# A hybrid Fourier/SSD transformer layer on Trainium2: PSUM tiles of the channel products, the DFT table's memory, and the opening of the last feed-forward block

## The chip, the cores and the metric

The kernel runs on one core of a Trainium2 chip (trn2). A core has five engines that work side by side, each through its own queue of instructions: TensorE (PE, matmuls, with its weight loads shown as PEld), VectorE (DVE), ScalarE (ACT), GpSimd (POOL) and SyncE (SP), which here issues the DMA transfers. The metric is the device time of one execution in microseconds (us); lower is better. The kernel before takes 2312.03 us, the median of three runs (2309.56, 2312.03 and 2312.89).

## The reference, cut to what matters

One layer works on 1024 latent tokens and 256 context tokens of width 1024, with the same weights for both, in float32:

```
def macaron_ffn(x, mod3, norm_pre, norm_post, w_gate, w_up, w_down):
    h = modulate(rms_norm(x, norm_pre), mod3[:, 0], mod3[:, 1])
    y = (jax.nn.silu(h @ w_gate) * (h @ w_up)) @ w_down
    return x + MACARON_WEIGHT * mod3[:, 2][:, None, :] * rms_norm(y, norm_post)

def mix_sublayer(...):
    h = modulate(rms_norm(x, norm_pre), mod3[:, 0], mod3[:, 1])
    u_f, z, xbc, dt_raw = jnp.split(h @ w_in, [...], axis=-1)
    xbc = centred_dwconv_silu(xbc, conv_w, conv_b)
    ...                                  # two directions of an SSD scan, y = y_f + flip(y_b) + ...
    out = jnp.concatenate([fourier_mix(u_f, fourier_w), y], axis=-1) @ w_out
    return x + mod3[:, 2][:, None, :] * rms_norm(out, norm_post), h_f, h_b

def fourier_mix(u, fourier_w):
    uh = u.reshape(b, L, FOURIER_HEADS, FOURIER_HEAD_DIM).astype(jnp.float32)
    f = jnp.fft.fft2(uh, axes=(1, 3), norm='ortho').real.astype(u.dtype)
    return jnp.einsum('blhd,hde->blhe', f, fourier_w).reshape(b, L, FOURIER_WIDTH)
```

The latent tokens pass a feed-forward block (hidden width 2816), the mixing block and a second feed-forward block. The context tokens pass the first feed-forward block and the mixing block's projection, which give the SSD scan its starting states. The vectors of `modulate` and the gates come from adaLN products of the two conditioning vectors.

## The kernel before, in words

**Precision.** A float32 product is taken as three products of halves in a faster format (fp32r): `split` (L194) casts the high half on ScalarE (L198) and subtracts it on VectorE for the low half (L199); `mm3` (L456) issues high times high, high times low and low times high. Nearly all matmuls of the trace therefore carry L461. The matmuls of the DFT (L1240) stay plain float32, and each of them shows as two in the trace.

**Order.** The code is written for a tile framework whose scheduler plays the program on a model of the engines and deals out each engine's queue from that; the queue that results can differ from the written order. Within an engine the queue is fixed. SBUF is handed out by an allocator of areas (`m.alloc`, `m.free`, `Ring` for areas used in turn) in several regions (F0, Q, X1, X2, R0; the trace shows them as F, Q1a, X3a, X3b, R and so on). A load into an area that had another use before waits for the last reader of that memory, so the place of an area sets how early a load can run. PSUM tiles are named by tags (`self.banks`): a product takes the next tile of its tag and waits until that one has been emptied.

**Stages, in the order of the program.**
- First feed-forward block (`ffn1`). The gate and up products are formed in units by a scheme of seven products per unit (`units`, `uload`, `usums`, `usplit`, `product`, `u_first`, `u_mid`, `u_late`, driven by `ffn_up`, L611). A unit loads raw weights (`uload`, L527), forms sums of them on VectorE (`usums`, L534 to L537) and splits them in three groups A11, S1 and S4 (`usplit`). The token side has such sums too: h^T of the latent tokens is held in blocks and sums of blocks. `ffn_down` (L669) then multiplies with the down weights for token tiles 0 and 1, then 2 to 4, then 5 to 7; `down_prep` (L654) loads and splits one group of down weights and gated activations ahead. After a token tile's last matmul comes its norm (`post`, L904, the last step at L793).
- Projection (`project`, L951). First the channel products: 24 blocks of 24 matmuls into `pch` tiles, emptied by ScalarE or VectorE. The banks are dealt out at L963, two one-bank tiles for tag GU and two for AUX beside two larger ones. Between the blocks the rest of the adaLN runs (`ada`, L699): 48 loads of 256 KB into a ring of three areas, sums over them on VectorE (L771), and for every eight loads a cast on ScalarE (L715) and a pair of `pmod` matmuls (L722, L723). Then come the token products `pz`.
- SSD and context (`ssd_and_ctx`, L1354): the scan over chunks of the latent tokens beside the context's feed-forward block, whose products (`gu`, `y`) fill TensorE between the scan's steps. The Fourier part (`fourier`, L1167) is stepped among them; its table for the last step of the DFT is loaded into one area of 4 x 1024 columns (`tw`) and is used at L1240. Then follow the context's norm and transposes (L806, L816), and its projection (`pdt`, `pch`).
- Mixing output (`mix_out`, L1510), where the blocks of h^T for the second feed-forward block are made and partly stored in DRAM (`h_d`).
- Second feed-forward block (`ffn2`, L1648). One pair of hidden blocks is done by plain gate and up products (`gu`), while the stored blocks of h^T are loaded back, summed on VectorE (L396 to L399) and split (L422). Then the units of `ffn_up` follow as in the first block, with products into `pa`, `pb`, `pc` and `pd`, and the last down product (`y`).

Of the kernel before, what the change touches and what calls it, by code (L numbers as in the profile page):

```python
# [7 lines left out]
F32 = mybir.dt.float32  # L8
# [3 lines left out]
ALU = mybir.AluOpType  # L12
AX = mybir.AxisListType

D = 1024
# [112 lines left out]
class Kernel:  # L128
# [423 lines left out]
    def product(self, u, p, steps=range(4)):  # L552
        m = self.m
        tag = {1: "A", 2: "A", 6: "B", 5: "C", 3: "C", 7: "D", 4: "D"}[p]
# [4 lines left out]
        for i in steps:  # L559
            lh, ll = self.wop(wop, i)  # L560
            rh, rl = (m.r(q) for q in self.hop[hop][i])
            self.mm3([P], lh, ll, [rh], [rl], p in (1, 6, 5, 7) and i == 0, i == 3, p != 6)
# [47 lines left out]
    def ffn_up(self, begun, tail, step=lambda: None):  # L610

        n = len(self.ulist)
        for u in range(n):
            if u or not begun:
# [19 lines left out]
            if u > (1 if begun else 0):  # L634
# [34 lines left out]
    def ffn_down(self, post, step=lambda p, f: None, before=lambda p: None):  # L669
# [12 lines left out]
        for p, ts in enumerate(self.passes):  # L682
            for fs in [(0, 1)] + [(f,) for f in range(2, NF - 2)] + [(NF - 2, NF - 1)]:
# [6 lines left out]
                for i, t in enumerate(ts):  # L690
# [141 lines left out]
    def ffn1(self):  # L832
# [71 lines left out]
        def post(t, P):  # L904
            self.rs = V if t > 5 else nc.gpsimd
# [8 lines left out]
        self.ffn_down(post, step, before)  # L914
# [36 lines left out]
    def project(self):  # L951
# [11 lines left out]
        self.banks(main=2, GU=2, AUX=2)  # L963
# [203 lines left out]
    def fourier(self):  # L1167
# [32 lines left out]
        m.free(bd, fw, cs, *u)  # L1200
        s = [m.alloc(256) for _ in range(4)]
        zr = []
        for c in range(2):
            zr.append(m.alloc(2048))
            pq3 = m.f(pq[c]).rearrange("p (t x) -> p t x", x=256)
            z4 = m.f(zr[c]).rearrange("p (r i q x) -> p r i q x", r=4, i=2, q=2)
            for i in range(2):
# [6 lines left out]
                flat = m.f(zr[c]).rearrange("p (r i x) -> p r i x", r=4, i=2)  # L1214
                G.tensor_tensor(out=flat[:, 0, i], in0=s02, in1=s13, op=ALU.add)
                G.tensor_tensor(out=flat[:, 2, i], in0=s02, in1=s13, op=ALU.subtract)
                dd, d1 = (q.rearrange("p (q x) -> p q x", q=2) for q in (d02, d13))
                V.tensor_tensor(out=z4[:, 1, i, 0], in0=dd[:, 0], in1=d1[:, 1], op=ALU.subtract)
                V.tensor_tensor(out=z4[:, 1, i, 1], in0=dd[:, 1], in1=d1[:, 0], op=ALU.add)
                V.tensor_tensor(out=z4[:, 3, i, 0], in0=dd[:, 0], in1=d1[:, 1], op=ALU.add)  # L1220
                V.tensor_tensor(out=z4[:, 3, i, 1], in0=dd[:, 1], in1=d1[:, 0], op=ALU.subtract)
# [3 lines left out]
        tw = m.alloc(4096)  # L1225
        for r in range(4):
            self.load(tw, a["dft"][r], 1024 * r, 1024 * r + 1024)
        fo = [m.alloc(1024, F32, self.F0) for _ in range(2)]
        yield
        for c in range(2):  # L1230
            z4 = m.f(zr[c]).rearrange("p (r i q x) -> p r i q x", r=4, i=2, q=2)
# [619 lines left out]
```

## Time and profile before

| what | value |
|---|---|
| median of three runs | 2312.03 us (2309.56 to 2312.89) |
| the profiled execution | 2308.27 us, its span 2306.3 us |
| mean granted TensorE clock | 0.974 of full speed |
| TensorE busy (PE) | 2151.5 us, 93% of the span |
| weight loads (PEld) | 1795.3 us, 78% |
| VectorE (DVE) | 1500.8 us, 65% |
| ScalarE (ACT) | 922.3 us, 40% |
| GpSimd (POOL) | 410.9 us, 18% |

Times inside the profile are microseconds from the start of the span. An engine is busy while one of its instructions runs; issuing a DMA is not counted. The granted clock is that of TensorE as the chip's throttle allowed it, 1 being full speed (2.4 GHz), 0.5 the lower level (1.2 GHz), and a value between the two a mean over a stretch. A wait is the idle time of an engine before an instruction, put down to what released that instruction last.

### The profile page before, as it was taken

Reading aid. Unit: us, or ns where it says so; the run is one execution under the profiler, and the core shown is the slowest. Engines: PE = TensorE matmul, PEld = TensorE weight load, DVE = VectorE, ACT = ScalarE, POOL = GpSimd, SP = SyncE. Lnnn points to the kernel's source line nnn. Section 1 sums busy time; section 2 is a strip of 40 time slices with the busy share of each in tenths; the row PEclk is TensorE's granted clock in tenths of the full one; section 3 lists DMA queues with packets and bytes.
Section 4 is the critical chain, followed back from the end, with each engine's and each line's share of the span. In section 5 each row is a group of like instructions: output and inputs, shape, how many; then the busy total and the mean of one; then the engine's idle time right before and its main releaser. Section 6 shows DMA issues by size and latency. Waiting matters only on the chain.

```text
span 2306.3 us, 28361 instructions
## 1 busy us (share of the span) xinstructions
PE 2151.5 (93%) x10532; PEld 1795.3 (78%) x10532; DVE 1500.8 (65%) x2231; ACT 922.3 (40%) x1403; POOL 410.9 (18%) x439
## 2 busy tenths in 40 slices
PE   5899999999999899989989978888799999999998
PEld 3688888888878899878878867676688888878886
DVE  6888887655555743358888857786655565656453
ACT  4332323235454414336555545355222222245341
POOL 0000000002030100026866631773000000001010
PEclk9999999999999999999999989999899999999999
DMA  6244444247665742123445445453422221258572
GB/s 263 89 128 135 137 133 135 78 165 257 201 205 175 218 126 92 60 77 106 137 145 167 127 157 165 152 175 121 137 76 91 74 85 68 88 190 285 173 231 89
DMA packets 124826, 329.38 MB, mean 143 GB/s; under 512 B 12928, under 2 KB 43776, under 8 KB 123664
## 3 DMA queue, kind: packets, MB, share of 16 engines
q1 hardware_dynamic: 124688, 327.57, 43.6%
q8 instruction: 83, 1.36, 0.2%
q14 instruction: 55, 0.45, 0.1%
HBM read 273.77 MB, written 53.76 MB: 142 GB/s over the span
## 4 chain that ended last, share of the span: by engine, by line
PE 72%; DVE 10%; DMA 8%; issue 4%; ACT 3%; POOL 3%; SPq 0%; DVEq 0%; POOLq 0%; ACTq 0%
PE y L461 21%; PE pa L461 10%; PE pc L461 10%; PE pd L461 10%; PE pb L461 5%; PE pch L461 5%; PE pz L461 3%; PE gu L461 3%; DMA X3b<-adaR 1%; DVE R L199 1%; PE pwo L461 1%; DVE F L1311 1%; DMA F<-ffn_w 1%; DMA X2a<-ada 1%; POOL R L1265 1%
## 5 line engine op out<-in xcount | busy, mean ns | idle before, releaser
L198 ACT CAST R<-F 128x1024 fp32r<-128x1024 f32 (+1 forms) x172 | 164.7, 963 | 258.2 <-PE pd L461 75.4
L199 DVE TENSOR_TENSOR R<-F,R 128x1024 fp32r<-128x1024 f32 (+1 forms) x155 | 194.7, 1260 | 92.5 <-ACT R L198 85.4
L207 POOL TENSOR_SCALAR F<-F 128x1 f32<-128x1 f32 x18 | 3.7, 206 | 1307.9 <-ACT F L228 1307.7
L198 ACT CAST Q1a<-F 128x1024 fp32r<-128x1024 f32 (+1 forms) x114 | 128.8, 1132 | 209.7 <-PE pd L461 85.8
L461 PE MATMUL pch<-R 128*128 128x512 f32 (+1 forms) x912 | 171.5, 347 | 11.2 <-DVE F L948 6.4
L461 PE MATMUL gu<-R 128*128 128x256 f32 (+1 forms) x1152 | 164.9, 302 | 8.8 <-DVE X5a L512 6.2
L461 PEld LDWEIGHTS pch<-R 128*128 128x128 f32 x912 | 147.1, 195 | 31.6 <-DVE F L948 5.3
L461 PEld LDWEIGHTS gu<-R 128*128 128x128 f32 x1152 | 153.1, 197 | 17.2 <-DVE X5a L512 7.3
L199 DVE TENSOR_TENSOR Q1a<-F,Q1a 128x1024 fp32r<-128x1024 f32 x92 | 112.3, 1221 | 33.7 <-ACT Q1a L198 33.1
L1265 POOL TENSOR_TENSOR R<-F 128x384 fp32r<-128x384 f32 x128 | 126.3, 1015 | 21.7 <-PE pD L1299 15.1
L461 PE MATMUL y<-Q1a 128*128 128x512 f32 x432 | 105.4, 392 | 0.7 <-DVE Q1a L199 0.3
L461 PE MATMUL pa<-R 128*128 128x512 f32 x306 | 86.6, 399 | 12.6 <-ACT R L198 12.1
L461 PEld LDWEIGHTS y<-Q1a 128*128 128x128 f32 x432 | 80.5, 188 | 18.8 <-DVE Q1a L199 0.8
L198 ACT CAST X7a<-F 128x1024 fp32r<-128x1024 f32 (+1 forms) x48 | 58.9, 1229 | 90.1 <-PE pd L461 78.4
L461 PE MATMUL pa<-R,Q1a 128*128 128x512 f32 x330 | 92.9, 394 | 0.0
L461 PE MATMUL y<-Q1a,X3a 128*128 128x512 f32 x348 | 86.8, 396 | 0.0
L461 PE MATMUL pc<-R,Q1a 128*128 128x512 f32 x286 | 85.3, 391 | 0.0
L461 PE MATMUL pd<-R,Q1a 128*128 128x512 f32 x286 | 84.0, 391 | 0.0
L461 PE MATMUL y<-X7a 128*128 128x512 f32 x330 | 79.4, 396 | 2.9 <-ACT X7a L198 2.9
L199 DVE TENSOR_TENSOR X7a<-F,X7a 128x1024 fp32r<-128x1024 f32 (+1 forms) x48 | 69.4, 1446 | 18.5 <-ACT X7a L198 17.6
L461 PEld LDWEIGHTS pa<-R 128*128 128x128 f32 x306 | 58.5, 192 | 27.0 <-ACT R L198 12.5
L534 DVE TENSOR_TENSOR F<-F 128x1024 f32<-128x1024 f32 x42 | 51.4, 1225 | 41.8 <-DMA F<-ffn_w 41.5
(427 smaller groups left out, 4922.2 us busy)
## 6 DMA issues: line engine op xcount, KB each, us to landing
F<-ffn_wd SPq DMA_DIRECT2D x154, 512.0 KB, 4.8
F<-ffn_w SPq DMA_DIRECT2D x42, 1024.0 KB, 5.4
X3b<-adaR SPq DMA_DIRECT2D x96, 256.0 KB, 2.8
F<-ffn_w SPq DMA_DIRECT2D x44, 512.0 KB, 4.2
F<-w_ch SPq DMA_DIRECT2D x26, 512.0 KB, 4.4
g_d<-X3b SPq DMA_DIRECT2D x22, 512.0 KB, 2.8
g_d<-F SPq DMA_DIRECT2D x20, 512.0 KB, 2.6
X3b<-g_d SPq DMA_DIRECT2D x44, 192.0 KB, 5.0
```

The lines of the kernel that those rows point to most:

```text
L198: nc.scalar.copy(out=m.r(hi, off, off + n), in_=m.f(src, soff, soff + n))
L199: (E or nc.vector).tensor_tensor(out=m.r(lo, off, off + n), in0=m.f(src, soff, soff + n), in1=m.f(hi, off, off + n), op=ALU.subtract)
L207: V.tensor_scalar(out=mv, in0=ss, scalar1=scale * RSQ_M, scalar2=EPS * RSQ_M, op0=ALU.mult, op1=ALU.add)
L461: self.nc.tensor.matmul(out=outs[c], lhsT=l, rhs=r[c], start=first and ps == 0, stop=last and ps == 2, skip_group_check=again)
L534: V.tensor_tensor(out=m.f(e).rearrange("p (s c) -> p s c", s=2), in0=s[1].unsqueeze(1).broadcast_to([128, 2, 512]), in1=m.f(w, 0, 2048).re ...
L1265: G.tensor_tensor(out=m.r(R, 384 * i, 384 * i + 384).rearrange("p (h l) -> p h l", h=3), in0=self.cst(tri).unsqueeze(1).broadcast_to([128, ...
L1311: V.scalar_tensor_tensor(out=w, in0=m.f(cb, 512 + 128 * g, 640 + 128 * g), scalar=self.dtT[:, c, 12 + h : 13 + h], in1=w, op0=ALU.mult, op ...
```

## The change

Four places are rewritten.

1. In the channel products the six banks that the two large tiles and GU held together become six one-bank tiles of tag GU (AUX keeps two). In the last pass of the first down product the token tiles of the first step are taken in the order 7, 5, 6, and the reciprocal root of tile 5's norm is computed on VectorE, where POOL did it before.
2. In the Fourier part the two operands of the DFT and its table are held in four pieces each. Two pieces of the table are loaded as soon as the first operands of the Fourier part are freed, the other two where memory of the SSD scan becomes free; the outputs `fo` move to region Q.
3. In the second feed-forward block the raw area of the first unit is allocated, and its load issued, ahead of the blocks of h^T that are read back. `h_sums` is written out in place, over 2560 columns where it used 3584. The first unit takes its products in the order 1, 2, 3, 6, 5, 7, 4, with product 3 in a tile of its own (tag AUX). Products 1, 2 and 3 are those that read h^T's own blocks and the sums of weights that go with them, and the rest read the sums of blocks.
4. Before the last down product three groups are prepared where two were, and the areas for them come from other places.

```
-        self.banks(main=2, GU=2, AUX=2)
+        self.banks(GU=6, AUX=2)
...
-            self.rs = V if t > 5 else nc.gpsimd
+            self.rs = V if t > 4 else nc.gpsimd
...
-        self.ffn_down(post, step, before)
+        self.ffn_down(post, step, before, 2)
...
         m.free(bd, fw, cs, *u)
+        tw = [m.alloc(1024) for _ in range(2)]
+        for r in range(2):
+            self.load(tw[r], a["dft"][r])
...
-            zr.append(m.alloc(2048))
+            zr.append([m.alloc(512) for _ in range(4)])
...
-        tw = m.alloc(4096)
-        for r in range(4):
-            self.load(tw, a["dft"][r], 1024 * r, 1024 * r + 1024)
-        fo = [m.alloc(1024, F32, self.F0) for _ in range(2)]
+        tw += [m.alloc(1024) for _ in range(2)]
+        for r in range(2, 4):
+            self.load(tw[r], a["dft"][r])
+        fo = [m.alloc(1024, F32, self.Q) for _ in range(2)]
...
-        hb = [m.alloc(3584, F32, F0) for _ in range(2)]
+        self.raw = Ring(m, 2560, 1, F32, F0)
+        self.units("ffn2", 1)
+        self.uload(0)
+        hb = [m.alloc(2560, F32, F0) for _ in range(2)]
...
-        self.raw = Ring(m, 2560, 2, F32, F0)
-        self.we = m.alloc(1024, F32, F0)
+        self.raw.areas.append(m.alloc(2560, F32, F0))
+        self.we = m.alloc(1024, F32, X2)
...
+            if u == 0 and not begun:
+
+                self.product(0, 1)
+                self.U[0] = self.ut.next()
+                U = self.m.f(self.U[0])
+                self.nc.scalar.copy(out=U, in_=self.P[0, "A"])
+                self.product(0, 2)
+                P3 = self.P[0, "X"] = self.psum("px", "AUX")
+                self.product(0, 3, tag="X")
...
-            self.down_prep()
-            self.down_prep()
+            self.graw.areas.append(m.alloc(384, F32, F0))
             self.down_begin("ffn2", ((0, 1), (2, 3, 4), (5, 6, 7)))
+            for _ in range(3):
+                self.down_prep()
```

TensorE's queue at the end of the channel products, from the fifth `pmod` pair on; `pch` is a channel product's tile, `pmod` the adaLN product's, `pz` the first token product's. Before:

```order
L461 MATMUL pch<-R_60 128x256 x7
L722 MATMUL pmod<-Q1a,R_60 128x512
L461 MATMUL pch<-R_60 128x256 x6
L723 MATMUL pmod<-Q1a,R_60 128x512
L461 MATMUL pch<-R_60 128x256 x35
L461 MATMUL pch<-R_60,X3a 128x256 x36
L722 MATMUL pmod<-Q1a,R_60 128x512
L461 MATMUL pch<-R_60,X3a 128x256 x6
L723 MATMUL pmod<-Q1a,R_60 128x512
L461 MATMUL pch<-R_60,X3a 128x256 x54
L461 MATMUL pz<-Q1a,R_60 128x408 x192
```

The same place after:

```order
L461 MATMUL pch<-R_60 128x256 x17
L755 MATMUL pmod<-Q1a,R_60 128x512
L461 MATMUL pch<-R_60 128x256 x6
L756 MATMUL pmod<-Q1a,R_60 128x512
L461 MATMUL pch<-R_60 128x256 x25
L461 MATMUL pch<-R_60,X3a 128x256 x47
L755 MATMUL pmod<-Q1a,R_60 128x512
L461 MATMUL pch<-R_60,X3a 128x256 x6
L756 MATMUL pmod<-Q1a,R_60 128x512
L461 MATMUL pch<-R_60,X3a 128x256 x43
L461 MATMUL pz<-Q1a,R_60 128x408 x192
```

The pairs of `pmod` stand further back among the channel products: 54 matmuls were left behind the last pair and 43 are now. At the first pair it is 110 matmuls ahead of it, where there were 101.

TensorE's queue at the DFT: `y` is the context's down product, `pdft` the DFT's tiles, `ptr` the transposes of the context's two token blocks, `pst` products of the scan's states, `pdt` the first product of the context's projection. Before:

```order
L1336 MATMUL pst<-Q4a 128x192 x4
L1240 MATMUL pdft<-Q4a,X5a 128x256 x15
L816 MATMUL ptr<-F_61 128x128 x8
L1240 MATMUL pdft<-Q4a,X5a 128x256 x15
L816 MATMUL ptr<-F_61 128x128 x8
L1240 MATMUL pdft<-Q4a,X5a 128x256 x2
L461 MATMUL pdt<-R_60 24x256
```

After:

```order
L461 MATMUL y<-R_60 128x512 x8
L1275 MATMUL pdft<-X5a 128x256 x5
L1275 MATMUL pdft<-F_61,X5a 128x256 x2
L1371 MATMUL pst<-Q4a 128x192
L1275 MATMUL pdft<-F_61,X5a 128x256 x2
L1371 MATMUL pst<-Q4a 128x192
L1275 MATMUL pdft<-F_61,X5a 128x256 x4
L1371 MATMUL pst<-Q4a 128x192 x2
L1275 MATMUL pdft<-X5a 128x256 x8
L1275 MATMUL pdft<-F_61,X5a 128x256 x4
L849 MATMUL ptr<-F_61 128x128 x8
L1275 MATMUL pdft<-F_61,X5a 128x256 x4
```

Three `pdft` matmuls (not shown) now stand among the `y` products ahead of these rows, and 28 of the 32 stand before the first row of transposes shown; the first two pieces of the table are in X5a and the others in F.

VectorE's queue at the opening of the last feed-forward block, where `gu` is a tile of the plain gate and up products. L396 to L399 are the sums of h^T before, L1707 to L1710 after, and the splits of them are L422 before and L199 (into X7a) after. Before:

```order
L422 TENSOR_TENSOR X7a<-F_61,X7a 128x2048
L1682 TENSOR_TENSOR F_61<-gu,F_61 128x512
L422 TENSOR_TENSOR X7a<-F_61,X7a 128x2048
L534 TENSOR_TENSOR F_61<-F_61 128x1024
L536 TENSOR_TENSOR F_61<-F_61 128x512
L537 TENSOR_TENSOR F_61<-F_61 128x512
L199 TENSOR_TENSOR R_60<-F_61,R_60 128x1024 x2
L534 TENSOR_TENSOR F_61<-F_61 128x1024
L199 TENSOR_TENSOR X7a<-F_61,X7a 128x1536
```

The same place after:

```order
L1708 TENSOR_TENSOR F_61<-F_61 128x512
L199 TENSOR_TENSOR R_60<-F_61,R_60 128x1024
L1709 SCALAR_TENSOR_TENSOR F_61<-F_61 128x512
L199 TENSOR_TENSOR R_60<-X7b,R_60 128x1024
L1707 TENSOR_TENSOR F_61<-F_61 128x512
L1727 TENSOR_TENSOR F_61<-gu,F_61 128x512
L1710 TENSOR_TENSOR F_61<-F_61 128x512
L1708 TENSOR_TENSOR F_61<-F_61 128x512
L1709 SCALAR_TENSOR_TENSOR F_61<-F_61 128x512
L1710 TENSOR_TENSOR F_61<-F_61 128x512
L199 TENSOR_TENSOR X7a<-F_61,X7a 128x2048 x2
L199 TENSOR_TENSOR X7a<-F_61,X7a 128x1536
```

The first unit's weight sums (L534 to L537) have moved up, before these rows, among the last transposes of the mixing output. Its two splits into R stood behind the last split of h^T and now stand among the last sums of h^T. The split of group S4 (1536 columns) still ends the stretch.

## Rows read from the trace of the kernel before

**Rows 1.** Busy time by stretch: start:end, us, busy us (instructions), PEclk, DMA share, GB/s.

```profile
753.00:844.00 91.00, 80.19 (x614) 77.58 (x615) 62.97 (x114) 29.57 (x60) 5.74 (x6) 0.94 0.64 197
1030.00:1340.00 310.00, 275.82 (x1796) 251.06 (x1796) 259.17 (x380) 173.73 (x308) 210.43 (x189) 0.95 0.42 135
1353.00:1380.00 27.00, 18.90 (x83) 15.81 (x82) 12.10 (x31) 15.94 (x26) 7.84 (x5) 0.81 0.66 207
1641.50:1659.30 17.80, 5.23 (x14) 3.72 (x15) 14.29 (x14) 6.45 (x8) 0.00 (x0) 0.62 0.43 136
2057.70:2289.50 231.80, 231.75 (x998) 188.60 (x999) 113.77 (x131) 91.01 (x129) 16.95 (x35) 0.99 0.63 201
```

**Rows 2.** Waits of PE, 749 to 844: waited for, us in total, times, longest.

```profile
PE pch L461 <- ACT F L992: 5.6, 2, 4.5
PE pch L461 <- DVE X3b L793: 3.9, 1, 3.9
```

**Rows 3.** Timeline of PE, channel products: start, us, instruction, count [idle before, releaser].

```profile
752.90 7.50 PE L461 MATMUL pch<-R 128*128 128x256 f32 x48 [3.87 <-DVE X3b L793]
...
802.92 5.92 PE L461 MATMUL pch<-R 128*128 128x256 f32 x48
...
840.87 3.08 PE L461 MATMUL pch<-R,X3a 128*128 128x256 f32 x24 [0.93 <-ACT X3b L995]
```

**Rows 4.** Timeline of DVE and ACT, 755 to 836.

```profile
757.47 1.28 DVE L793 SCALAR_TENSOR_TENSOR X3b<-y,F,X3b 128x1024 f32<-128x1024 f32 x1 [2.88 <-DMA x_d<-X3b]
...
774.40 0.62 ACT L715 CAST Q1a<-F 128x512 fp32r<-128x512 f32 x1 [1.88 <-DVE F L771]
...
834.32 0.62 ACT L715 CAST Q1a<-F 128x512 fp32r<-128x512 f32 x1 [4.02 <-DVE F L771]
```

**Rows 5.** Timeline of all engines at the DFT, 1348 to 1381.

```profile
1348.94 0.32 SPq L1325 DMA_DIRECT2D y_d<-F  x1
...
1359.04 9.51 PE L1240 MATMUL pdft<-Q4a,X5a 128*128 128x256 f32 x30 [5.84 <-DMA Q4a<-dft]
...
1362.50 1.15 ACT L806 ACTIVATE F<-X5a,F 128x1024 f32<-128x1024 f32 x1 [0.61 <-DVE F L214]
...
1369.26 6.64 PE L1240 MATMUL pdft<-Q4a,X5a 128*128 128x256 f32 x30
...
1375.74 1.04 PE L816 MATMUL ptr<-F 128*128 128x128 f32 x8
...
1379.89 0.30 PE L461 MATMUL pdt<-R 128*24 128x256 f32 x1 [2.25 <-ACT R L828]
```

**Rows 6.** Timeline of PE and DVE at the last block's opening, 1630 to 1662.

```profile
1630.08 11.40 PE L461 MATMUL gu<-R,X7a 128*128 128x512 f32 x48
...
1636.46 0.69 DVE L396 TENSOR_TENSOR F<-F 128x512 f32<-128x512 f32 x1 [6.09 <-DMA F<-h_d]
...
1644.59 2.28 DVE L422 TENSOR_TENSOR X7a<-F,X7a 128x2048 fp32r<-128x2048 f32 x1
...
1652.88 2.35 DVE L199 TENSOR_TENSOR R<-F,R 128x1024 fp32r<-128x1024 f32 x2
...
1653.59 1.22 PE L461 MATMUL pa<-R 128*128 128x512 f32 x2 [12.11 <-ACT R L198]
...
1655.29 3.92 PE L461 MATMUL pa<-R 128*128 128x512 f32 x10 [0.48 <-DVE R L199]
...
1656.29 1.75 DVE L199 TENSOR_TENSOR X7a<-F,X7a 128x1536 fp32r<-128x1536 f32 x1
...
1660.43 1.57 PE L461 MATMUL pb<-X7a,R 128*128 128x512 f32 x6
```

**Rows 7.** A link of the chain that ended last: start, us, what.

```profile
1644.11 6.09 DMA F<-ffn_w
```

**Rows 8.** Timeline of PE at the start of the last down product.

```profile
2057.74 7.27 PE L461 MATMUL y<-X7a 128*128 128x512 f32 x24 [2.87 <-ACT X7a L198]
```

**Rows 9.** Longest wait of PE, 1030 to 1340.

```profile
PE gu L461 <- DVE X5a L512: 6.2, 1, 6.2
```

More of the change, by code (lines that the diff above doesn't have):

```diff
@@ L550, in wop, with product @@
         return [self.m.r(q, o, o + 128) for q in self.wq[g]]
-    def product(self, u, p, steps=range(4)):
+    def product(self, u, p, steps=range(4), tag=None):
         m = self.m
-        tag = {1: "A", 2: "A", 6: "B", 5: "C", 3: "C", 7: "D", 4: "D"}[p]
+        tag = tag or {1: "A", 2: "A", 6: "B", 5: "C", 3: "C", 7: "D", 4: "D"}[p]
         if p in (1, 6, 5, 7) and steps[0] == 0:
@@ L613, in ffn_up @@
         for u in range(n):
-            if u or not begun:
+            if u == 0 and not begun:
[6 more added lines that the diff above has]
+                self.product(0, 3, tag="X")
+                V = self.nc.vector
+                s, d = self.u_dest(0)
+                self.u_end(0, 0, s, d)
+                self.product(0, 6)
+                V.tensor_tensor(out=U, in0=self.P[0, "B"], in1=U, op=ALU.add)
+                self.usums(1)
+                self.usplit(1, "A11")
+                for p in (5, 7):
+                    self.product(0, p)
+                self.u_mid(0)
+                V.tensor_tensor(out=self.m.f(d[1]), in0=self.P[0, "C"], in1=U, op=ALU.add)
+                V.tensor_tensor(out=self.m.f(d[1]), in0=P3, in1=self.m.f(d[1]), op=ALU.add)
+                self.u_end(0, 1, s, d)
+                self.product(0, 4)
+                V.tensor_tensor(out=self.m.f(d[2]), in0=self.P[0, "D"], in1=U, op=ALU.add)
+                self.u_end(0, 2, s, d)
+                self.usplit(1, "S1")
+                self.usplit(1, "S4")
+                self.uload(2)
+                continue
+            if u:
                 for p in (1, 6):
@@ L667, in down_prep, with ffn_down @@
         self.ready[q] = (wh, wl, gh, gl)
-    def ffn_down(self, post, step=lambda p, f: None, before=lambda p: None):
+    def ffn_down(self, post, step=lambda p, f: None, before=lambda p: None, turned=0):
         m = self.m
@@ L689, in ffn_down @@
                     self.down_prep()
-                for i, t in enumerate(ts):
+                order = list(enumerate(ts))
+                if p == 2 and fs[0] == 0:
+                    order = order[turned:] + order[:turned]
+                for i, t in order:
                     for f in fs:
@@ L1714, in ffn2 @@
             r.release()
-        m.free(self.cc, wb, lb, h0, l0, h1, l1, *(x for q in T[1:] for x in q), *(m.sub(x, 768, 1280) for x in T[0]))
-        self.pairs(Q, 2, 0)
-        self.pairs(X1, 3, 4)
-        self.graw.areas += [m.alloc(384, F32, X2) for _ in range(2)]
+        m.free(self.cc, wb, lb, h0, l0, h1, l1, *(x for q in T[2:] for x in q),
+               *(m.sub(x, o, n) for q, o, n in ((0, 0, 512), (0, 1664, 384), (1, 0, 512), (1, 1536, 512)) for x in T[q]))
+        self.pairs(R0, 2, 0)
+        self.pairs(X1, 2, 3)
+        self.graw.areas.append(m.alloc(384, F32, X2))
         x = Ring(m, 1024, 2, F32, F0)
```

42 lines of the change are left out of this document (23 added, 19 removed).

## The prediction, made before the changed kernel ran

> **What bounds the kernel now.** I read the page's list by engine first (TensorE is busy 93% of the span), then busy time by stretch, then the waits of TensorE in the stretches where it is not full, and last the timeline there. The reader is to see in the stretches that TensorE is full where the two feed-forward blocks run in steady state (231.75 of 231.8 us in the last one) and is not full in four places: the channel products of the projection, the state-space part, the DFT with the context's last norm, and the opening of the last feed-forward block [rows 1]. Only there can the edits give anything; no matmul is taken away, so the whole effect is idle TensorE time, and the slow clock behind it.
>
> **The change part by part.**
>
> *First channel products (L963 before).* Six one-bank tiles in place of two. TensorE waits here 5.6 us for ACT and 3.9 for DVE to empty tiles [rows 2]. With six tiles these waits can go; that the tiles now taken first are token tile 5's, and that its reciprocal root is computed on VectorE, lets the first product start near 749.0, where TensorE now falls idle (752.90 less 3.87 [rows 3]). But what ends last is another chain: the adaLN vectors, 48 loads through a ring of three buffers into VectorE sums. Its casts for the modulation products come at 774.40 for the first and 834.32 for the sixth [rows 4], so one every (834.32 - 774.40)/5 = 12.0 us. A channel product's matmul takes 5.92/48 = 0.123 us [rows 3], and 71 to 87 of them stand between two modulation pairs in either order, 10.7 us at most. TensorE is therefore ahead of that chain already, and will be further ahead: 110 matmuls (13.5 us) now stand before the first pair, so it gets there about 11 us early and waits. The stretch ends with the last pair plus what stands behind it: 54 matmuls before, 43 now, 11 x 0.123 = 1.35 us, and the wait of 0.93 for a tile inside them [rows 3] goes. The chain's own start hangs on VectorE's normalisation of tile 7, which ends at 757.47 + 1.28 [rows 4] and frees the ring's first buffer; tile 5 is ready earlier, but VectorE now has 21 more small operations in between, so I move it by 0.5 at most. Value: **3 us**. Upper bound, if nothing but TensorE counted: 614 instructions [rows 1] x 0.123 = 75.5 us from 749.0, so 824.5 against 843.95 (840.87 + 3.08 [rows 3]): 19.4 us. Lower bound: -2, were the chain's start 2 us later.
>
> The granted clock is 0.81 in the stretch after the 5.84 us DFT wait and 0.62 after the 12.11 us one [rows 1, 5, 6], and 48 channel matmuls took 7.50 us after an idle 3.87 where later ones took 5.92 [rows 3]. The Trainium skill, *TensorE: Matmul & The Clock Gate* (Part 1: The HAM clock gate), says that the half clock is the default and that sustained activity releases the full one; the traces agree. It speaks against this edit, because the new 11 us wait ends at the half clock. By the rows that is 1.6 us per such wait, beside slack of 12.0 - 10.7 = 1.3 in one period and more in the next, so I add nothing; were it never made up, the edit would give 1.4 instead of 3.
>
> *DFT table in four pieces (L1217, L1238).* TensorE now stands 5.84 us for the table, then runs the DFT with the second transposed context block behind it: that block's input is ready at 1362.50 + 1.15 = 1363.65, its transposes run at 1375.74, and the next product starts at 1379.89 after 2.25 more us [rows 5]. Now two pieces are loaded into other memory as soon as the first DFT operands are free, and 3 of the 32 DFT matmuls stand inside the context's down product. The last piece still waits, since its memory holds the output tile whose store is issued at 1348.94 [rows 5], and it stands behind that store and a context load in SP's queue. With 6.1 us for the store's end and the load (6.09 is the duration of a load twice as large [rows 7]) it lands near 1355. Behind it stand 20 DFT matmuls, two rows each in the trace, at 6.64/30 = 0.221 [rows 5]: 8.9 us, and one set of transposes, 1.04: 1365, and 1.3 us for the three matmuls put earlier: 1366.3, which is 9.4 before 1375.74. What follows is fed by weight loads through three raw buffers of which these transposes free two, so I take a little over half: **5.5 us**. Upper bound 1375.74 - 1363.65 = 12.1; lower bound -1.3, if only the three matmuls in the way remain.
>
> *Opening of the last FFN (L1660 to L1725).* The last gate/up product of the first pair ends at 1630.08 + 11.40 = 1641.48; the first channel-unit product starts 12.11 us later, because its raw weights are loaded only then, and its last ten matmuls take 3.92 us at the slow clock [rows 6]; the second product ends at 1660.43 + 1.57 = 1662.00. Now that load (6.09 us [rows 7]) is issued before the blocks of h^T are read back, so product 1 can start at 1641.5. The next in TensorE's order is product 3, which needs group S4's split, and S4 is written over the operands of the product that ends at 1641.48. VectorE's order decides when: the sums of h^T start at 1636.46 and their last split ends at 1644.59 + 2.28 = 1646.87 [rows 6]; two splits of unit 0, 2.35 us [rows 6], now stand in between, and S4's, 1.75 us [rows 6], behind: 1651.0. What else is queued: on SP the early load stands before the last two stores of h^T, on VectorE the first weight sum stands before the last eviction of a transposed block, so each late microsecond of that load delays those stores, the loads behind them and the sums. I add 1.5: 1652.5. Ten matmuls at the slow clock, 3.9, end product 3 at 1656.4, the second product of the unit, 5.6 before 1662.00. Value: **5.5 us**. Upper bound: S4 split at once, two steps of 1.75, 1645.0, and ten matmuls at 11.40/48 = 0.24: 1647.4, so 14.6. Lower bound: a second load's length, 6.1 - 1.5 late: 1.0; and -1 with the six modified products in a worse order.
>
> *Three groups prepared ahead in the down product (L1722).* Removes up to 2.87 us, the one wait of that stretch [rows 8]. The third group's split runs beside the last unit, where TensorE is full. Value **2 us**, bounds -1 and 2.9.
>
> *Order of the first down step of the first FFN (tile 7 first).* The same 18 matmuls; nothing by itself.
>
> *Order elsewhere.* The tile scheduler has also re-dealt the state-space part, with the same instructions. TensorE idles 310.0 - 275.82 = 34.2 us there [rows 1], the longest wait is 6.2 [rows 9]; I take 0, and 6.2 to both sides.
>
> Sum: 3 + 5.5 + 5.5 + 2 = 16 us. The profiled execution took 2308.27, so 2292.3; the median of the three runs, 2312.03, lies 3.8 above it, and the forecast against it is **2296.0 us**.
>
> **The rivals.**
> 1. *The tiles were the bound of the channel products.* For it: 9.5 us of waits on tiles [rows 2]. Against it: the even 12 us step of the modulation casts [rows 4]. It gives 19.4 in place of 3: 2279.6. Chance 0.10.
> 2. *The opening closes whole*, with VectorE's queue no hindrance: 14.6 in place of 5.5, 2286.9. For it: VectorE idles 6.09 us before 1636.46 [rows 6], where the new work could stand; against it: in the new order one of the sums waits ahead of it. Chance 0.20.
> 3. *The loads come no sooner where it counts*: the early weight load and the last DFT piece both wait for memory that is freed late; the middle two terms fall to 0, 5 us remain: 2307.0. Chance 0.13.
> 4. *The re-dealt state-space part loses more than the rest gains.* Its place is 1030 to 1340, its price one longest wait, 6.2 us [rows 9], for each of the points where POOL's, VectorE's and TensorE's new orders don't meet; from three such waits beyond today's (18.6 > 16) the kernel is slower. With four: 2312.0 - 16 + 24.8 = 2320.8. For it: three engines are above two thirds busy there [rows 1]; against it: the rows moved are few matmuls each. Chance 0.05.
>
> **How the numbers follow.** The forecast has the remaining 0.52. Runs of this kernel differ by some 0.2% (4.6 us), so "same" is 2307.4 to 2316.6. Rival 4 is the slower case, 0.05. The same case is part of rival 3 and of bad luck in the state-space part: 0.10. The rest, 0.85, is faster. The range reaches from 28 us of gain (rival 2 with a good term elsewhere) to 6: 2284 to 2306; the forecast's own range is 2290 to 2302.
>
> **What would show it.** Right: a TensorE wait of some 10 us before the first modulation product and token products (pz) starting 2 to 5 us sooner after the y products; the second context transposes 7 to 10 us sooner relative to the end of the context's y; a rest of some 5 to 10 us idle inside products 1 and 3 instead of 12.11, ended by S4's VectorE split; no wait in the down stretch. Wrong: token products sooner by over 10 us (rival 1), px without a wait (rival 2), DFT matmuls still waiting over 5 us on a DMA (rival 3), or more than 40 us of TensorE idle time in the state-space part (rival 4).

## The result, and the profile after

The changed kernel takes 2283.41 us, the median of four runs (2281.11 to 2286.04), against 2312.46 (2309.56 to 2315.78, four runs) before. The ratio is 0.9874, with a 95% interval of 0.9857 to 0.9892: 29 us faster. The forecast was 2296.0 with a range from 2284 to 2306, so the direction was right, the time lies just below the range, and the gain is almost twice as large as forecast. The profiled executions took 2308.27 and 2281.11.

I cut both spans at points that TensorE passes in every version: the end of the first block's `y`, the first `pz`, the first `pD` (state-space part), the end of the context's `y`, the first `pwo`, the first `y` of the last down product, and the end. The context's DFT, norm and projection stand in one row, and so do the mixing output and the last block's units, because their inner border moves when work is dealt out in another order.

| stretch, us | before | after | difference | forecast |
|---|---|---|---|---|
| start to end of first `y` | 749.0 | 748.2 | -0.8 | 0 |
| channel products | 94.8 | 89.8 | -5.0 | -3 |
| token products | 198.3 | 198.4 | +0.1 | 0 |
| state-space part | 306.8 | 296.3 | -10.4 | 0 |
| DFT, context's norm and projection | 88.9 | 83.1 | -5.8 | -5.5 |
| mixing output, last block's units | 608.7 | 608.4 | -0.3 | -5.5 |
| last down product | 259.8 | 255.0 | -4.8 | -2 |

The state-space part gave the most, although the change rewrites nothing there but the pieces of the Fourier part that are stepped among its products. Busy time by stretch of the changed kernel, which answers to [rows 1] (columns as there; the second row is the state-space part, and the last the same length of the last down product):

```profile
748.00:838.00 90.00, 76.72 (x613) 74.78 (x613) 68.05 (x134) 32.36 (x64) 2.98 (x2) 0.94 0.67 207
1036.40:1332.70 296.30, 276.98 (x1831) 251.59 (x1832) 248.32 (x370) 173.01 (x309) 207.40 (x186) 0.98 0.44 141
1332.70:1359.40 26.70, 18.31 (x84) 14.81 (x82) 14.84 (x39) 17.15 (x30) 7.20 (x5) 0.89 0.68 227
1623.40:1641.00 17.60, 10.36 (x31) 7.51 (x30) 14.38 (x15) 6.14 (x5) 0.00 (x0) 0.71 0.47 150
2030.70:2262.50 231.80, 231.80 (x1007) 188.79 (x1006) 112.98 (x129) 92.09 (x130) 15.99 (x35) 1.00 0.63 203
```

The same state-space stretch, cut at the same points, in the kernel before:

```profile
1042.10:1348.80 306.70, 279.37 (x1824) 254.62 (x1824) 251.80 (x367) 172.50 (x308) 205.09 (x186) 0.96 0.41 131
```

TensorE's busy time fell by 2.4 us, and its idle time from 306.7 - 279.4 = 27.3 to 296.3 - 277.0 = 19.3. Its three costliest waits there, before and then after (waited for, us in total, times, longest):

```profile
PE gu L461 <- DVE X5a L512: 6.2, 1, 6.2
PE pst L1336 <- DVE Q4a L1343: 4.8, 2, 2.6
PE pyd L1322 <- DVE F L1324: 2.9, 2, 1.9
```

```profile
PE pst L1371 <- DVE Q4a L1378: 4.0, 2, 3.5
PE y L461 <- ACT R L198: 3.7, 3, 3.1
PE pst L1371 <- ACT Q4a L1376: 2.8, 1, 2.8
```

The 6.2 us wait of [rows 9] is gone. It ended with VectorE's emptying of a context tile (L512), and the place where that happens shows why it was late. The engines there before, with rows left out (start, us, engine, line, out<-in, count, idle time and its releaser):

```profile
1145.59 4.29 PE L461 MATMUL y<-R 128*128 128x512 f32 x18
...
1151.12 4.16 DVE L1311 SCALAR_TENSOR_TENSOR F<-X5a,F 128x128 f32<-128x128 f32 x5
...
1151.36 1.64 PE L1299 MATMUL pD<-R 128*128 128x384 f32 x8
...
1151.86 0.83 POOL L1265 TENSOR_TENSOR R<-F 128x384 fp32r<-128x384 f32 x1 [1.08 <-PE pD L1299]
...
1152.80 2.34 POOL L199 TENSOR_TENSOR R<-F,R 128x1024 fp32r<-128x1024 f32 x1
1155.09 6.06 POOL L1265 TENSOR_TENSOR R<-F 128x384 fp32r<-128x384 f32 x7
1155.21 1.18 DVE L1312 TENSOR_TENSOR F<-F 128x384 f32<-128x384 f32 x1
...
1156.31 1.75 DVE L1311 SCALAR_TENSOR_TENSOR F<-X5a,F 128x128 f32<-128x128 f32 x2
1157.98 1.21 DVE L512 TENSOR_TENSOR X5a<-y,X5a 128x1024 f32<-128x1024 f32 x1
1159.24 3.14 PE L461 MATMUL gu<-R 128*128 128x256 f32 x13 [6.24 <-DVE X5a L512]
```

And after:

```profile
1140.73 4.29 PE L461 MATMUL y<-R 128*128 128x512 f32 x18
...
1146.27 1.39 DVE L1346 SCALAR_TENSOR_TENSOR F<-X5a,F 128x128 f32<-128x128 f32 x5
...
1147.58 0.54 DVE L1347 TENSOR_TENSOR F<-F 128x384 f32<-128x384 f32 x1
...
1148.05 0.60 DVE L1346 SCALAR_TENSOR_TENSOR F<-X5a,F 128x128 f32<-128x128 f32 x2
...
1148.23 2.39 PE L1334 MATMUL pD<-R 128*128 128x384 f32 x8 [1.48 <-ACT F L1339]
1148.58 1.21 DVE L512 TENSOR_TENSOR X5a<-y,X5a 128x1024 f32<-128x1024 f32 x1
...
1148.72 2.45 POOL L1300 TENSOR_TENSOR R<-F 128x384 fp32r<-128x384 f32 x3 [2.79 <-PE pD L1334]
...
1150.42 1.91 PE L461 MATMUL gu<-R 128*128 128x256 f32 x8
```

VectorE runs the same instructions in the same order. Before, POOL starts in their midst, and five multiply-adds take 4.16 us (0.83 each). After, the `pD` products wait 1.48 us for ScalarE, POOL idles 2.79 us behind them, and the five take 1.39 (0.28 each). With the three instructions behind them (L1312 and two of L1311, after L1347 and two of L1346) it is 4.16 + 1.18 + 1.75 = 7.1 us before and 1.39 + 0.54 + 0.60 = 2.5 after. From the start of `y` to the next `gu`: 13.65 us before, 9.69 after, so 4.0 us at this one place.

Of the other three places, the channel products and the opening look as forecast. TensorE's timeline there, with VectorE's row of the last two splits of h^T and that of group S4 (answers to [rows 3] and [rows 6]):

```profile
756.79 7.53 PE L461 MATMUL pch<-R,X3a 128*128 128x256 f32 x62
773.56 0.80 PE L755 MATMUL pmod<-Q1a,R 128*128 128x512 f32 x1 [9.24 <-ACT Q1a L748]
...
1612.10 11.40 PE L461 MATMUL gu<-R,X7a 128*128 128x512 f32 x48
1623.34 2.88 PE L461 MATMUL pa<-R 128*128 128x512 f32 x12
...
1628.48 6.16 DVE L199 TENSOR_TENSOR X7a<-F,X7a 128x2048 fp32r<-128x2048 f32 x3
1631.92 1.22 PE L461 MATMUL px<-R,X7a 128*128 128x512 f32 x2 [5.69 <-ACT X7a L198]
1634.69 4.63 PE L461 MATMUL px<-R,X7a 128*128 128x512 f32 x10 [1.55 <-DVE X7a L199]
```

The waits named in the prediction stand there: 9.24 us before the first modulation product, and 5.69 + 1.55 us inside product 3. The first of these two ends with ScalarE's half of S4's split (the cast), the second with VectorE's. At the DFT (answers to [rows 5]) the table's last piece is waited for 0.39 us in place of 5.84, the second transposes stand at 1352.24, and a new wait of 6.02 us, for ScalarE's casts of the context block, stands behind them. Ahead of those casts VectorE has waited 3.27 us for POOL, which was still splitting the first block. So the second transposes came 7.4 us sooner behind the end of the context's `y` (19.5 us, 26.9 before), and the product after them only 4.4 (26.6, 31.1 before):

```profile
1337.65 1.99 PE L1275 MATMUL pdft<-F,X5a 128*128 128x256 f32 x8 [0.39 <-DMA F<-dft]
...
1352.24 1.09 PE L849 MATMUL ptr<-F 128*128 128x128 f32 x8
...
1355.32 0.41 DVE L856 TENSOR_SCALAR F<-ptr,F 128x128 f32<-128x128 f32 x1 [3.27 <-POOL R L862]
...
1359.36 0.41 PE L461 MATMUL pdt<-R 128*24 128x256 f32 x1 [6.02 <-ACT R L861]
```

### The profile page after: what moved, and what is told of

The parts are those of the page before. It is cut to its first block, busy times and chain, and to the rows that moved or that the text cites. A ratio compares the mean times of both kernels' runs of the same rounds, so it can differ in the third digit from the quotient of the medians.

```text
span 2279.3 us, 28369 instructions
## 1 busy us (share of the span) xinstructions
PE 2142.1 (94%) x10532; PEld 1785.8 (78%) x10532; DVE 1501.4 (66%) x2246; ACT 922.8 (40%) x1403; POOL 406.2 (18%) x425
## 5 line engine op out<-in xcount | busy, mean ns | idle before, releaser
L199 DVE TENSOR_TENSOR R<-F,R 128x1024 fp32r<-128x1024 f32 (+1 forms) x153 | 193.4, 1268 | 92.0 <-ACT R L198 85.3
L199 DVE TENSOR_TENSOR Q1a<-F,Q1a 128x1024 fp32r<-128x1024 f32 x92 | 112.2, 1221 | 35.1 <-ACT Q1a L198 34.5
L1300 POOL TENSOR_TENSOR R<-F 128x384 fp32r<-128x384 f32 x128 | 128.5, 1034 | 22.5 <-PE pD L1334 15.9
L198 ACT CAST X7a<-F 128x1536 fp32r<-128x1536 f32 (+4 forms) x45 | 54.5, 1216 | 112.2 <-PE pd L461 78.3
L461 PEld LDWEIGHTS y<-Q1a 128*128 128x128 f32 x432 | 80.6, 188 | 19.3 <-DVE Q1a L199 1.4
L461 PE MATMUL pa<-R 128*128 128x512 f32 x306 | 84.5, 392 | 0.0
L199 DVE TENSOR_TENSOR X7a<-F,X7a 128x1536 fp32r<-128x1536 f32 (+4 forms) x45 | 64.2, 1430 | 23.7 <-ACT X7a L198 23.6
L461 PE MATMUL y<-R,Q8a 128*128 128x512 f32 x336 | 78.3, 390 | 0.0
L461 PEld LDWEIGHTS y<-Q1a,X3a 128*128 128x128 f32 x348 | 65.4, 188 | 15.5
L461 PE MATMUL y<-R 128*128 128x512 f32 x264 | 70.1, 408 | 4.9 <-ACT R L198 3.7
```

The source lines that it names most:

```text
L198: nc.scalar.copy(out=m.r(hi, off, off + n), in_=m.f(src, soff, soff + n))
L199: (E or nc.vector).tensor_tensor(out=m.r(lo, off, off + n), in0=m.f(src, soff, soff + n), in1=m.f(hi, off, off + n), op=ALU.subtract)
L461: self.nc.tensor.matmul(out=outs[c], lhsT=l, rhs=r[c], start=first and ps == 0, stop=last and ps == 2, skip_group_check=again)
L1300: G.tensor_tensor(out=m.r(R, 384 * i, 384 * i + 384).rearrange("p (h l) -> p h l", h=3), in0=self.cst(tri).unsqueeze(1).broadcast_to([128, ...
```

## The experiments

The stretches, as cut above, in all of them:

| kernel | median us | ratio to before (95%) | channel | state-space | DFT + context | mixing + units | last down |
|---|---|---|---|---|---|---|---|
| before | 2312.46 | 1 | 94.8 | 306.8 | 88.9 | 608.7 | 259.8 |
| after | 2283.41 | 0.9874 (0.9857 to 0.9892) | 89.8 | 296.3 | 83.1 | 608.4 | 255.0 |
| only_dft | 2310.41 | 1.0003 (0.9992 to 1.0014) | 94.9 | 310.4 | 83.4 | 610.6 | 259.9 |
| only_banks | 2297.82 | 0.9947 (0.9934 to 0.9960) | 90.5 | 295.7 | 89.4 | 611.9 | 259.8 |
| only_open | 2306.35 | 0.9984 (0.9971 to 0.9996) | 94.3 | 307.4 | 88.4 | 606.0 | 260.8 |
| only_tail | 2304.59 | 0.9977 (0.9968 to 0.9986) | 95.8 | 302.7 | 88.6 | 612.4 | 256.2 |
| only_rs | 2298.21 | 0.9942 (0.9927 to 0.9956) | 89.8 | 298.5 | 89.6 | 611.4 | 259.4 |
| gu_turned | 2309.53 | 0.9993 (0.9981 to 1.0005) | 93.7 | 305.8 | 87.0 | 613.5 | 260.4 |
| after_no_rs | 2299.22 | 0.9943 (0.9928 to 0.9959) | 93.0 | 312.7 | 83.5 | 607.3 | 254.9 |
| no_dft | 2287.38 | 0.9896 (0.9880 to 0.9911) | 91.5 | 293.5 | 90.3 | 606.8 | 255.0 |
| after_ring | 2286.30 | 0.9895 (0.9880 to 0.9910) | 90.2 | 301.8 | 87.1 | 606.6 | 255.0 |
| only_open2 | 2304.43 | 0.9972 (0.9960 to 0.9983) | 96.0 | 302.7 | 88.3 | 604.8 | 257.8 |

Each row of stretches is from one profiled execution; each ratio is to runs of the kernel before on the same chip, whose medians lay between 2310.4 and 2312.5. The run `port`, below, is the kernel before with a block behind its end; its state-space part took 305.5 us.

**Each part alone.** Four kernels take one part of the change each. In `only_open` the down product's second pair of operands lies over those of the last unit's product 4, which is thereby changed; `only_open2`, below, has other areas.

only_dft: the hunks of `fourier`.

> The kernel before with the DFT edit alone (table and operands in four pieces, outputs in the other region). The changed kernel was 10.4 us shorter between the first state-space product and the context's last y matmul (296.3 against 306.8) and 4.4 us shorter from there to the context's projection (26.6 against 31.1), though the change rewrites nothing in the first of the two. Theory A: the shorter state-space part comes from the DFT edit, which makes the scheduler deal TensorE's, VectorE's and POOL's queues out anew there: the state-space stage 295 to 299, the DFT stage 26 to 28, the kernel 13 to 16 us faster (2296 to 2299). Theory B: it comes from the channel products, whose earlier end shifts the two streams against each other: state-space stage 304 to 308, DFT stage 26 to 28, 3 to 6 us faster. Theory C: the stage varies from run to run: any value, not that of either kernel.

only_banks: `GU=6`, `turned=2` and `t > 4`.

> The kernel before with the edits of the channel products alone (six one-bank tiles, last pass of the first down product beginning with tile 7, tile 5's root on VectorE). Both theories: the stage from the end of the first block's y to the first token product goes from 94.8 to 89.8, as in the changed kernel. Theory A (state-space gain from the DFT edit): the rest unchanged within 2 us although the order there differs, 4 to 6 us faster in all. Theory B (state-space gain from this edit): state-space stage about 296, 14 to 16 us faster. Theory C: any value.

only_open: the new order of the first unit and the early `uload(0)`.

> The kernel before with the edits of the last feed-forward block's opening alone (raw load of unit 0 ahead of the blocks of h^T, products 1, 2, 3 first), the two groups ahead of the down product as before. The queue of TensorE in the state-space part is that of the kernel before. Theories A and B: state-space stage 306 to 308, mixing output unchanged or up to 4 us longer (the changed kernel was 4.0 us longer there), opening and units 4 to 5 us shorter (405.0 to about 400.5): 0 to 5 us faster. If the 4.0 us of the mixing output come from this edit, that stage is 207 to 208 here; if from the other edits, 203 to 204. Theory C: state-space stage anywhere.

only_tail: three `down_prep` and the areas for them.

> The kernel before with three groups prepared ahead of the last down product where two were, and areas for them, alone. If the 2.87 us wait is all that the stall costs: last stage 259.8 to 257, 2.9 us faster. If the granted clock behind the wait costs as well (0.93 over 23.6 us before, 1.00 after): 255, 4.5 to 5 us faster. All other stages within 0.5 us of before, the state-space stage too (theories A and B); off by more in theory C.

Theory A fell: with the DFT edit alone the state-space part was not shorter (310.4, of which 1.5 are the DFT matmuls dealt into it). It was 295.7 with the channel edits alone, as theory B had said. But theory B also had 3 to 6 us of gain for only_dft, and that kernel gained nothing that can be measured. The tail gave 3.6 us of stretch, more than the 2.87 of the wait. The 4.0 us more of mixing output that the text on only_open asks about belong to no edit: cut at the last gate/up matmul, that part takes 203.7 us before, the lowest of the old openings, and 204.8 in only_open, within the 203.6 to 207.7 that eleven of the twelve profiles of the table show. The opening with the units behind it takes 405.0 before, 401.1 in only_open and 400.8 in the changed kernel.

**Which of the channel edits, and by what way.** Two theories were left: the order that the scheduler deals out (now put down to the channel edits), or an earlier end of the channel products. In the texts of these three runs the first is theory A and the second theory B. I split the edits in two, and took one of them back in the changed kernel.

```
only_rs:      -            self.rs = V if t > 5 else nc.gpsimd
              +            self.rs = V if t > 4 else nc.gpsimd
gu_turned:    -        self.banks(main=2, GU=2, AUX=2)
              +        self.banks(GU=6, AUX=2)         # and the tiles of the last pass as 7, 5, 6
after_no_rs:  the changed kernel with  self.rs = V if t > 5 else nc.gpsimd
```

> The kernel before with one edit: the reciprocal roots of token tile 5 on VectorE where POOL computed them. TensorE's queue in the state-space part is then, row for row, that of the kernel with all three channel edits (whose stage was 295.7 against 306.8); the two one-bank tiles and the order 5, 6, 7 of the last down pass are as before. Theory A (the order that the scheduler deals out decides the stage): state-space stage 294 to 299. Theory B (it is shorter because six tiles let the channel products end earlier against the loads and the clock): state-space stage 304 to 309. For the channel stage: 94 to 95.5 if the two tiles are its bound, 90 to 91 if the root's way from POOL to VectorE gave the five.

> The kernel before with six one-bank tiles and the last down pass beginning with tile 7, and the roots of tile 5 still on POOL. TensorE's queue in the state-space part is that of the kernel before. Theory A: state-space stage 302 to 309, kernel 2 to 5 us faster from the channel stage alone (90 to 92 against 94.8). Theory B: state-space stage 294 to 299, 12 to 16 us faster.

> The changed kernel with the roots of tile 5 back on POOL, and everything else as changed. Its state-space queue is that of the kernel with the DFT edit alone (stage 310.4, of which 1.5 are the DFT matmuls dealt into it). Theory A: state-space stage 304 to 311, 9 to 13 us slower than the changed kernel, 2293 to 2297. Theory B: 294 to 299, and the time within 3 us of the changed kernel's 2283.4.

One number in one line decides. With it alone the kernel gains 0.58% (0.44 to 0.73), and without it the changed kernel loses 15.8 us, more than the 9 to 13 expected. It moves 14 instructions of one column each from POOL to VectorE at about 745 to 756 us; the scheduler then deals the state-space part out differently, some 290 us later. The queues of TensorE, VectorE, ScalarE and POOL in that part are the same, row for row, in before, only_open, only_tail, gu_turned, only_open2 and port, and again in only_banks, only_rs and no_dft; the DFT edit changes some rows of either order (the same ones in only_dft and after_no_rs, and in after and after_ring). Seven profiles with the old order there have 302.7 to 311.2 us (the 1.5 us of DFT matmuls taken off where they stand in it, mean 306.5), and five with the new order 293.5 to 300.3 (mean 296.6): 9.9 us apart, and the two groups do not overlap. Nor does TensorE's idle time in that part: 26.9 to 28.4 us with the old order (mean 27.5), 18.2 to 22.5 with the new one (mean 20.2). That is 7.3 of the 9.9 us; the rest is busy time of the same matmuls, at a granted clock of 0.95 to 0.98 and of 0.97 to 0.99. Where the channel products end is not what decides: in only_banks and in after_no_rs the first token product starts at the same 842.3 us, and the state-space part then takes 295.7 in the one and 312.7 in the other. Six tiles and the turned order together gave no more than 2 us of their stretch, and nothing in the whole time that can be told from no change, where 2 to 5 us were expected. TensorE's waits in the state-space part of only_rs and then of gu_turned:

```profile
PE y L461 <- ACT R L198: 3.6, 2, 3.1
PE pst L1336 <- DVE Q4a L1343: 3.5, 2, 2.7
...
PE pD L1299 <- ACT F L1304: 2.7, 3, 1.5
```

```profile
PE gu L461 <- DVE X5a L512: 6.2, 1, 6.2
PE pst L1340 <- DVE Q4a L1347: 4.7, 2, 2.7
```

The first two of only_rs are, within 0.5 us, waits of the changed kernel, and it has no wait of 6.2 us; those of gu_turned are the waits of the kernel before.

**The disputed cost by itself.** A block behind the end of the kernel before:

```
+        stt(cb)              # 12 x V.scalar_tensor_tensor(out=w, in0=cb, scalar=k, in1=w), 128x128
+        V.tensor_copy(...)   # POOL's products below wait for this
+        rows()               # 12 x G.tensor_tensor(128x384)
+        stt(cb)
...
+        rows()               # alone
...
+        stt(P)               # in0 in PSUM, alone
+        V.tensor_copy(...)
+        rows()
+        stt(P)
```

> The kernel before, with a block behind its end that measures one cost by itself: 12 multiply-adds of VectorE on 128x128 f32 in SBUF alone; the same beside 12 products of POOL on 128x384 (the state-space part's forms); the POOL products alone; and the multiply-adds with one operand in PSUM, alone and beside POOL. In the changed kernel five such multiply-adds took 1.39 us (0.28 each) where POOL was idle, and before, at the same place, 4.16 us (0.83 each) where POOL was busy. Theory P (VectorE is slowed by POOL working on SBUF): 0.25 to 0.30 us alone, 0.75 to 0.90 beside POOL, and POOL about 0.8 to 0.85 in both. Theory Q (the difference has another cause, as a wait for ScalarE within the group): 0.25 to 0.30 in both. With an operand in PSUM: 0.3 to 0.4 beside POOL if only two SBUF operands are slowed, over 0.7 if any access to SBUF is.

```profile
2306.93 3.42 DVE L1854 SCALAR_TENSOR_TENSOR mw<-mcb,mk,mw 128x128 f32<-128x128 f32 x13
...
2310.33 8.66 DVE L1854 SCALAR_TENSOR_TENSOR mw<-mcb,mk,mw 128x128 f32<-128x128 f32 x11
2310.50 9.96 POOL L1859 TENSOR_TENSOR mR<-mg,mk 128x384 fp32r<-128x384 f32 x12 [19.36 <-DVE mk L1863]
...
2320.79 9.44 POOL L1859 TENSOR_TENSOR mR<-mg,mk 128x384 fp32r<-128x384 f32 x12
...
2330.45 3.45 DVE L1854 SCALAR_TENSOR_TENSOR mw<-mP,mk,mw 128x128 f32<-128x128 f32 x13
...
2333.88 2.93 DVE L1854 SCALAR_TENSOR_TENSOR mw<-mP,mk,mw 128x128 f32<-128x128 f32 x11
2334.11 9.45 POOL L1859 TENSOR_TENSOR mR<-mg,mk 128x384 fp32r<-128x384 f32 x12 [3.88 <-DVE mk L1870]
```

Alone a multiply-add takes 3.42/13 = 0.26 us, beside POOL 8.66/11 = 0.79, as long as one of POOL's products (0.79 alone, 0.83 here): they take turns. With one operand in PSUM it is 0.27 alone and 2.93/11 = 0.27 beside POOL. Theory P holds (one run). The Trainium skill, *SBUF — State Buffer* (Who interferes with whom), has the rule: a VectorE instruction with two SBUF inputs contends with a GpSimd instruction that reads SBUF, and one with at most one SBUF input doesn't, apart from the two-port modes that it names. These rows agree.

**What was left of the other parts.**

no_dft: the changed kernel without the hunks of `fourier`. after_ring: `ring.areas.append(ring.areas.pop(0))` behind the ring of the adaLN loads. only_open2: only_open with `gring` at columns 512 and 896 of `T[0]`.

> The changed kernel with the Fourier part as before (table in one area, loaded late), everything else as changed. In the changed kernel the stage from the context's last y matmul to its projection took 26.6 us (31.1 before), but the DFT edit alone on the kernel before left its time the same within 0.1%: 4.4 us less there, and as much more in the stages ahead of it. Theory D (the DFT edit is worth its stage in the changed kernel): DFT stage 30 to 32, state-space stage 1.5 us shorter (no DFT matmuls in it), kernel 3 to 5 us slower than the changed one, 2286.5 to 2288.5. Theory E (what it gives there is lost beside it, in a wait for the context's norm): DFT stage 28 to 28.5, as with the channel edits alone, the kernel within 2 us of 2283.4.

> The changed kernel with the three areas of the adaLN ring taken in turn from the second on, so that the first weight block goes into an area that is free early (the second and third were loaded at 736.6 and 738.8, the first at 757.5, when the norm of tile 7 had freed its memory). TensorE's queue in the state-space part stays that of the changed kernel. Theory C1 (the end of the channel stage is set by the adaLN chain, whose start hangs on that load): first modulation product 2 to 4 us sooner (it stood 25.5 us behind the first channel product), its wait of 9.2 us shorter by as much, stage 86 to 88.5 in place of 89.8, the other stages the same within 2 us, kernel 1 to 4 us faster. Theory C2 (VectorE's rate through the sums, not their start, is the bound): stage 89 to 90.5. The state-space stage 294 to 299 in both, if its length goes by the order.

> The kernel before with the edits of the last feed-forward block's opening alone, the two groups ahead of the down product in areas that are free by then. State-space queue as before. TensorE starts the first unit's first product without a wait and then waits 5 to 6 us for the split of group S4: mixing output and units together 4 to 6 us below what the kernels with the opening of before took (608.7 in the one profile of before, 610.6 to 613.5 in five others), so 605 to 608, and 3 to 5 us faster in all. If the early load of the weights delays the blocks of h^T more than it gives: 609 or more, and no gain.

Without the DFT edit the changed kernel is 4.0 us slower by the medians, in the range of theory D, though the DFT's own stage came to 28.2 as in theory E, and the rest is in the context's projection. The four times of each do not overlap (2286.51 to 2288.69, and 2281.11 to 2286.04), but they are from two chips, the intervals of the ratios do overlap, and after_ring, which has the edit, was 1.1 us faster than no_dft on the same chip. So the size is uncertain. The DFT edit alone, on the kernel before, gave nothing that can be measured, although its stretch was 5.5 shorter: with the old state-space order and the DFT matmuls dealt into it, that part took longest of all (308.9 and 311.2, the 1.5 us taken off). TensorE idles no longer there than in the others with the old order (28.4 and 26.9 us); it is busy for longer. Why is open.

after_ring gave no gain, and its stage, 90.2, is theory C2's. The first cast did come sooner, 21.4 us behind the end of `y` in place of 24.7, as theory C1 had it. But the first modulation product stands 25.1 us behind the first channel product (25.5 in the changed kernel), because the wait now ends with ScalarE's emptying of a transpose's tile:

```profile
776.34 0.79 PE L755 MATMUL pmod<-Q1a,R 128*128 128x512 f32 x1 [9.36 <-ACT X3b L854]
```

An earlier load alone does not help there: two chains end at about the same time. Later the sixth cast is still 1.7 us sooner (81.1, and 82.8 in the changed kernel), but 61 channel matmuls now stand behind the last modulation pair, where the changed kernel has 43. The state-space part took 301.8 us, above the 294 to 299 expected, in the slowest of the four runs. No kernel beat the changed one.

The opening: the stretch of mixing output and units has a mean of 606.6 in the six profiles with the new opening, and of 611.4 in the six with the old one (608.7, the profile before, is the lowest of them). That is 4.8 us, which the table of the result hides; from the last gate/up matmul on it is 4.2 in the two profiles compared (405.0 and 400.8).

## Why the prediction was wrong

- **Order elsewhere (taken as 0, with 6.2 to both sides): the step that failed.** The part gave 9.9 us. I bounded it by the longest single wait. But it holds some 27 us of idle time, and with the new order 7.3 us of that went. The place of the 6.2 us wait accounts for 4.0 of the 9.9. That VectorE was late there because its multiply-adds ran beside POOL's products is borne out by the rows side by side and by the port run, though a kernel that takes away only this overlap wasn't tried. The other 6 us are spread over small waits and the clock (granted 0.96 before, 0.98 after), and which instruction moved each of them isn't separated; nor is it known why one root on another engine makes the scheduler find the better order. That it came out shorter and not longer is luck of the scheduler, and no term of the sum foresaw it. Rival 4 had this place right and its sign wrong.
- **First channel products (3):** 5.0. The place and the new wait were as forecast (9.24 against "some 10"), and rival 1, 19.4 us, fell. But the sum put the gain down to the tiles and the turned order as much as to the root, and those two alone gave little (gu_turned, 93.7): only_rs, the root alone, has all five, without that long wait. In the four kernels with the root on VectorE and the ring as before, 43 matmuls stand behind the last modulation pair and the sixth cast comes 82.3 to 84.5 us behind the end of `y`; in before, gu_turned and after_no_rs it is 54 matmuls and 84.7 to 85.4 us. The 11 matmuls and the 0.93 us wait were in the sum. That the chain of casts itself would end sooner (82.8 against 85.3) was not; the last of the three norms ahead of it, at whose end the sum had it begin, starts only 0.5 us sooner.
- **DFT (5.5):** 5.8 in the profile before against after, less 1.5 for the matmuls moved ahead; some 4.0 by no_dft in the whole time, and nothing measurable in only_dft. About right in size, but only together with the new state-space order, and partly by luck: the transposes came 7.4 us sooner where the sum had 9.4, and what was lost behind them went into the wait for POOL's splits (3.27), where the sum had blamed the weight loads.
- **Opening (5.5):** 4.8 by the means. Group S4's split ended at 1628.48 + 6.16 = 1634.64, that is 11.1 us behind the last gate/up matmul (1612.10 + 11.40 = 1623.50); the sum had 1652.5 - 1641.5 = 11.0 for it. Rival 2 fell: VectorE's queue was the hindrance.
- **Three groups ahead (2, at most 2.9): mis-sized.** It gave 4.8 in the profiles before and after, 3.6 in only_tail, where a wait of 0.9 for a norm is left, and 4.5 by the means (259.7 in the seven profiles without it, 255.2 in the five with it). The wait of 2.87 is not the whole price: the 24 matmuls behind it took 7.27 [rows 8], and 24 in the same product take 5.64 to 5.65 at the full clock in these rows of the changed kernel, so 1.6 more stood in a row that I had quoted.

```profile
2024.26 5.64 PE L461 MATMUL y<-R,Q8a 128*128 128x512 f32 x24
...
2032.46 5.65 PE L461 MATMUL y<-X7a 128*128 128x512 f32 x24
```

- **Order of the first down step (nothing):** right, as far as gu_turned, which holds it, tells.

The sum of what was measured is 9.9 + 5.0 + 4.0 + 4.8 + 4.5 = 28.2, against 29.1 in the medians. Without the state-space part it is 18.3, and the forecast had 16. Each alone on the kernel before, the four parts (with only_open2 for the opening) gain -0.03, 0.53, 0.28 and 0.23%, together 23 us; the intervals are too wide to tell whether the rest comes from their meeting.

## What to carry to other kernels

Where a scheduler deals out the queues, an edit of a few tiny instructions can re-deal a stretch hundreds of microseconds away, and that may be worth more than all the work meant to be improved. So compare the queues of every stretch in which the tightest engine waits, and price a re-dealt one by the sum of its waits, not by the longest. Look there for an instruction that has two durations: here it marked two engines in each other's way. An order that keeps them apart helped; an operand in PSUM, which no kernel here tried in the state-space part itself, may do the same. And price a wait of TensorE together with the slow matmuls right behind it.

## What the runs showed of the hardware

- VectorE's multiply-add of two SBUF operands (128x128 f32) takes 0.26 us alone and 0.79 beside POOL's products, one of each in turn; with one operand in PSUM it takes 0.27 beside POOL.
- The same state-space queue took 302.7 to 307.4 us in six profiles (before, only_open, only_tail, gu_turned, only_open2 and port). TensorE's idle time was the same within 0.6 us (27.2 to 27.7) and its busy time was not (275.0 to 280.0), with a granted clock of 0.98 where it was shortest and 0.96 where it was longest. In only_tail:

```profile
1041.70:1344.30 302.60, 275.06 (x1824) 249.96 (x1824) 252.21 (x367) 172.53 (x308) 206.97 (x186) 0.98 0.42 133
```

So a single profile tells such a stretch to some 5 us only.
